# A weight sum formed by an accumulating DMA, one split moved ahead of the other work, and attention's first weights spread over earlier steps

## The chip, the cores and the metric

One core of a Trainium2 chip runs the whole program. The metric is device time in microseconds of that core. Most of the time is spent by TensorE (PE) on matrix products; VectorE (DVE), ScalarE (ACT) and GpSimd (POOL) prepare operands and add up results, SyncE's queue (SP) and POOL's and ACT's queues issue the DMAs.

## The reference

Two sequences of 512 tokens with 1024 features go through two layers. Layer 0 mixes tokens by a Fourier transform, layer 1 by attention; each is followed by an MLP with a squared ReLU:

```python
for i in range(DEPTH):
    if i % 2 == 0: x = x + fourier_mix(rms_norm(x, fourier_norm), fourier_w_out)
    else:          x = x + gqa_attention(rms_norm(x, attn_norm), w_qkv, ..., w_o)
    a = maximum(rms_norm(x, mlp_norm[i]) @ w_up[i], 0)      # 1024 -> 4096
    x = x + (a * a) @ w_down[i]                             # 4096 -> 1024, "second product"
return rms_norm(x, final_norm)
```

Everything is float32.

## The kernel before, in words

**Three matmuls for one.** A float32 operand is split into two parts of a narrower type: ACT rounds the value to the high part (line 85, `CAST`), DVE subtracts to get the low part (line 86). A product is then three matmuls, high by high, high by low and low by high (line 784 for the MLPs; lines 80 to 82 elsewhere).

**Seven products for eight.** The MLP matrices are cut into 2 x 2 blocks, and a block product is made from seven products of sums of blocks in place of eight. In the second product of a layer (`second_product`) the hidden features lie in four groups of blocks (`g`), the outputs in four (`m`). For each pair (g, m) there is one `Row` (two products, with the plain weight blocks 11 and 12) and one `Sums` (five products: t1 with weight sum s1, t3 with s3, t2 with s2, b22 with s4, t4 with block 22). A product is 12 matmuls of 128x512, or 6 in the one group of layer 1 that has two blocks in place of four.

With a11, a12, a21, a22 the four weight blocks, the sums are s1 = a21 + a22, s2 = s1 - a11, s3 = a11 - a21, s4 = a12 - s2. `Sums.load` brings two raw tiles, x = (a12, a21) and y = (a11, a22). `sum_123` (lines 1058 to 1060) makes s1 and s2 in a third raw tile and s3 in place; `sum_4` (line 1066) makes s4 in place. `split_12` splits s1 and s2 as one tile, `split_4` splits s4, and `split_3` splits s3 and a22 as one tile.

**Items.** The main loop runs over 16 items (rows, sums), one for each (g, m), and mixes in work for the next item. Most items have one row besides the sums, 84 matmuls; the items of (0,0) (whose rows run ahead of the loop), (0,1), (3,2) and (3,3) have none, 60 matmuls. PE's order is written out by hand (`manual_schedule(engines={PE})`). The order of the other engines is fixed when the program is built, by a planner that puts an instruction where its operands and its buffer should be there, the earlier in the program first. Within an item the program says: the row's first product; load of the next row; `split_3` of this item's own sums; t1, load of the next sums; t3, the row's second product, split of the next row; t2, then `sum_123` and `split_12` of the next sums; b22, then `sum_4` and `split_4` of the next sums; t4; and at the end `finish`, which adds the parts up (lines 1129, 1130).

**Buffers.** Raw tiles share five buffers (`rawp`), split weights four (`wp`), and 38 buffers (`act`) hold the activations: 8 for the residual stream, 28 for the seven operands of a group (b11, b21, b22, t1 to t4, four each), which leaves two. Operands come back from memory where the first product spilled them (`fetch`, line 981), and `put` splits them; `change` fetches the next group's operand after its last use.

**End of layer 0.** When the last group is done for a value of m, `ready(m)` scales the result into attention's operand `hT` (`make_h`: ACT line 89, DVE line 90; one `act` buffer for each of four calls) and squares it for the norm (ACT line 160, POOL line 162). Attention's first weights, the four tiles `w_qkv[2, 0..3]` that make keys and values, are loaded and split by `late()` while the last items run. Each takes a raw buffer until it is split, and two `act` buffers. `late()` loads two of them at the start of item (3,2) and two at the start of item (3,3). Attention's first products use hT and these weights.

**Start of a layer's second product.** The first product's last step runs the generator `ahead()`, which fetches the first group's operands and loads the first four rows and the first sums by SP, while POOL still writes the last spills.

Of the kernel before, what the change touches and what calls it, by code (L numbers as in the profile page):

```python
# [11 lines left out]
F32 = mybir.dt.float32  # L12
# [3 lines left out]
ALU = mybir.AluOpType  # L16
AX = mybir.AxisListType

P = 128
# [18 lines left out]
GROUPS = ((0, 4), (4, 4), (8, 4), (12, 4)), ((2, 4), (6, 4), (10, 2), (12, 4))  # L38
# [5 lines left out]
def trunk_kernel(ctx, tc, x_in, xt_in, y_out, dcos, dsin, feat, rope, gfour, gcol, grow, gfin,  # L44
                 w_four, w_nyq, w_qkv, w_o, w_up, w_row2, w_row4, w_sum2, w_sum4, w_down):
    nc = tc.nc
# [3 lines left out]
    rawp = ctx.enter_context(tc.tile_pool(name="rawp", bufs=5))  # L50
# [9 lines left out]
    def nm(s):  # L60
        n_[0] += 1
        return f"{s}_{n_[0]}"

    def slot(shape, dt):
        return act.tile(shape, dt, tag="u4", name=nm("u"))

    def tm(shape=(P, 512), dt=F32):
        return tmp.tile(list(shape), dt, tag="t2", name=nm("t"))

    def small(n=4):  # L70
        return sm.tile([P, n], F32, tag="s", name=nm("s"), padded_shape=[P, 8])
# [12 lines left out]
    def split(dst_hi, dst_lo, src, eng=nc.vector):  # L84
        nc.scalar.copy(dst_hi, src)  # L85
        eng.tensor_sub(dst_lo, src, f32(dst_hi))  # L86
# [5 lines left out]
    def load_raw(src, shape=(P, 1024)):  # L92
        raw = rawp.tile(list(shape), F32, tag="raw", name=nm("raw"))
        nc.sync.dma_start(raw, src)
        return raw
# [17 lines left out]
    def load_w(src, eng=nc.vector, parts=1, home=own):  # L113
        raw = load_raw(src)
        w = home()
        for i in range(parts):
            sl = slice(i * 1024 // parts, (i + 1) * 1024 // parts)
            split(w[0][:, sl], w[1][:, sl], raw[:, sl], eng)
        return w
# [852 lines left out]
    def second_product(l, blocks, rows, late=lambda: None, ready=lambda m: None):  # L972
# [3 lines left out]
        def fetch(op, g, n):  # L976

            h = []
            for k in range(0, n, 2):
                hi, lo = slot([P, 2, 512], F32R), slot([P, 2, 512], F32R)  # L980
                nc.sync.dma_start(f32(lo), spill[l][op][g][k : k + 2].rearrange("n p f -> p n f"))
                h.append((hi, lo))
            return h

        def put(op, h):
            for hi, lo in h:
                split(hi, lo, f32(lo))
            b[op] = b.get(op, []) + [(hi[:, i], lo[:, i]) for hi, lo in h for i in range(2)]
# [11 lines left out]
        def residual(q, m):  # L1000
            if (q, m) not in there:
                xs[q, m] = slot([P, 2, 512], F32)
                nc.sync.dma_start(xs[q, m], park[q, m])
                there.add((q, m))
            return xs[q, m]
# [8 lines left out]
        def sums_raw(m, g, n):  # L1014
            if (1, m, g) in early:
                return early[1, m, g]
            w = w_sum4[GROUPS4.index((l, g)), m] if n == 4 else w_sum2[m]
            return [load_raw(w[:, i : i + 2], (P, 2, n * P)) for i in (0, 2)]

        class Row:  # L1020


            def __init__(self, m, g, n):
                self.m, self.g, self.n = m, g, n

            def load(self):
                residual(0, self.m)
                self.raw = None if self.m in rows_early else row_raw(self.m, self.g, self.n)
# [15 lines left out]
        class Sums:  # L1044


            def __init__(self, m, g, n):
                self.m, self.g, self.n, self.o = m, g, n, {}

            def load(self):  # L1050
                for q in range(NSEQ):
                    residual(q, self.m)
                self.x, self.y = sums_raw(self.m, self.g, self.n)

            def sum_123(self):
                a21, a11, a22 = self.x[:, 1], self.y[:, 0], self.y[:, 1]
                s = self.s = rawp.tile([P, 2, self.n * P], F32, tag="raw", name=nm("raw"))
                nc.vector.tensor_add(s[:, 1], a21, a22)
                nc.vector.tensor_sub(s[:, 0], s[:, 1], a11)
                nc.vector.tensor_sub(a11, a11, a21)  # L1060

            def split_12(self):
                self.s2, self.s1 = halves(self.s, self.n * P, (own, narrow)[self.n == 2])
# [62 lines left out]
        def finish(m):  # L1126
            left[m] -= 1
            if left[m] == 0:
                nc.vector.tensor_add(xs[0, m][:, 1], xs[0, m][:, 1], e[m])
                nc.vector.tensor_add(xs[1, m], xs[1, m], e[m].unsqueeze(1).broadcast_to([P, 2, 512]))  # L1130
                ready(m)
# [13 lines left out]
        def change(op, g):  # L1145

            if g + 1 < len(GROUPS[l]):
                later.append([0, op, g + 1, fetch(op, g + 1, GROUPS[l][g + 1][1])])

        rows, sums = items[0]  # L1150
        items[0] = [], sums
        with tc.manual_schedule(engines={ET.PE, ET.Activation, ET.DVE}):
            for r in rows:
                r.load()
                r.split()
            sums.load()
            rows[0].first()
            rows[1].first()
            put(*there_later[0])
            sums.sum_123()  # L1160
            sums.sum_4()
            rows[2].first()
            rows[3].first()
            for r, step in zip(rows, (sums.split_12, sums.split_4, sums.split_3, lambda: None)):
                r.second()
                step()
            for r in rows:
                finish(r.m)

        def hook():  # L1170
            for x in later:
                x[0] += 1
            if later and later[0][0] > 2:
                _, op, g, h = later.pop(0)
                b.pop(op, None)
                put(op, h)
                held[op] = g

        for k, (rows, sums) in enumerate(items):
            nrows, nsums = items[k + 1] if k + 1 < len(items) else ([], None)  # L1180
            if sums.g == len(GROUPS[l]) - 1 and sums.m > 1:
                late()
            with tc.manual_schedule(engines={ET.PE}):
                for r in rows:
                    r.first()
                    if r.m == 3:
                        change("b11", r.g)
                for r in nrows:
                    r.load()
                if k:  # L1190
                    sums.split_3()
                hook()
                for i, op in enumerate(("t1", "t3", "t2", "b22", "t4")):
                    sums.go(i)
                    if sums.m == 3:
                        change(op, sums.g)
                    if i == 0 and nsums:
                        nsums.load()
                    if i == 1:
                        for r in rows:  # L1200
                            r.second()
                            if r.m == 3:
                                change("b21", r.g)
                        hook()
                        for r in nrows:
                            r.split()
                    hook()
                    if k == 0 and i in (2, 4):
                        change(ROW[i // 4], 0)
                    if i == 2 and nsums:  # L1210
                        nsums.sum_123()
                        nsums.split_12()
                    if i == 3 and nsums:
                        nsums.sum_4()
                        nsums.split_4()
            for r in rows:
                finish(r.m)
            finish(sums.m)


    hT, rs, wkv = [[], []], [], []
# [5 lines left out]
        rs.append(r)  # L1227

    def late():
        for _ in range(2):  # L1230
            wkv.append(load_w(w_qkv[2, len(wkv)], home=lent))

    def ready(m):
        for q in range(NSEQ):
# [3 lines left out]
            put_away(q, m)  # L1238

    second_product(0, blocks, rows, late, ready)  # L1240

    gb = tm((P, 4, HD))
# [115 lines left out]
    for cg in (2, 0, 1):  # L1358
        ws = wkv if cg == 2 else [load_w(w_qkv[cg, u], home=own if u < 2 else lent) for u in range(4)]
        for q in range(NSEQ):  # L1360
# [6 lines left out]
            for t in range(NT if (cg, q) != (1, 1) else 2):  # L1367
# [11 lines left out]
                if cg == 2:  # L1379
                    raw = tm((P, 256))  # L1380
# [3 lines left out]
                else:  # L1384
                    raw = tm()
# [7 lines left out]
    raw, ss = slot([P, 1024], F32), small(8)  # L1393
# [30 lines left out]
    for kh in range(2):  # L1424
        ahead += [load_w(w_o[k], home=lent) for k in range(len(ahead), 4 * kh + 4)]
        ws = ahead[4 * kh :]
        for q in range(NSEQ):
            if kh == 0:
                load_xs(q, park[q])
            for fo in range(KC):  # L1430
# [13 lines left out]
                if (q, fo) > (1, 4):  # L1444
                    blocks.first_lo(fo - 5)
    blocks.first_lo(3)
    second_product(1, blocks, ())
    ats = []
    for f in range(2 * PLAIN):
        raw = load_raw(plain[f], (P, 2, 512))  # L1450
# [263 lines left out]
```

## Time and profile before

| | us |
|---|---|
| median of 3 runs | 1725.88 (1724.98 to 1727.17) |
| the profiled execution | 1728.54 |
| its span, first to last instruction | 1726.8 |
| PE busy in the span | 1677.5 (97%) |
| DVE busy | 1260.5 (73%) |
| ACT busy | 865.7 (50%) |
| POOL busy | 349.3 (20%) |

Times in the rows are microseconds from the start of the span. A matmul's busy time in the profile covers its way through the array, so that neighbours overlap; how fast PE really goes is seen from how many matmuls start in a stretch. A row of the timeline has the start, the length, the engine, the line, the operation, the tiles (out<-in), the count, and in brackets how long the engine stood idle before it and what released it.

### The profile page before, as it was taken

Reading aid. Unit: us, or ns where it says so; the run is one execution under the profiler, and the core shown is the slowest. Engines: PE = TensorE matmul, PEld = TensorE weight load, DVE = VectorE, ACT = ScalarE, POOL = GpSimd, SP = SyncE. Lnnn points to the kernel's source line nnn. Section 1 sums busy time; section 2 is a strip of 40 time slices with the busy share of each in tenths; the row PEclk is TensorE's granted clock in tenths of the full one; section 3 lists DMA queues with packets and bytes.
Section 4 is the critical chain, followed back from the end, with each engine's and each line's share of the span. In section 5 each row is a group of like instructions: output and inputs, shape, how many; then the busy total and the mean of one; then the engine's idle time right before and its main releaser. Section 6 shows DMA issues by size and latency. Waiting matters only on the chain. (4 is left out here: it accounts for less than half of the span.)

```text
span 1726.8 us, 21966 instructions
## 1 busy us (share of the span) xinstructions
PE 1677.5 (97%) x7846; PEld 1393.1 (81%) x7846; DVE 1260.5 (73%) x1871; ACT 865.7 (50%) x1530; POOL 349.3 (20%) x312
## 2 busy tenths in 40 slices
PE   4999999999999999999999999999999999999997
PEld 4888888888788888788887888788888887888887
DVE  8778777555878869975578844697765578879865
ACT  6666444445442435546687724564444562434334
POOL 3330444222000000412234302102432210000004
PEclk8999999999999999999999999999999999999999
DMA  8833455349654545430100212224543593535322
GB/s 282 220 111 122 153 203 199 141 155 343 257 189 153 195 146 197 154 107 25 49 25 1 90 57 98 110 102 166 195 172 140 203 399 123 201 130 214 137 98 98
DMA packets 103350, 266.06 MB, mean 154 GB/s; under 512 B 10169, under 2 KB 10169, under 8 KB 103241
## 3 DMA queue, kind: packets, MB, share of 16 engines
q1 hardware_dynamic: 86760, 231.63, 37.3%
q10 hardware_dynamic: 14112, 25.70, 3.9%
q0 software_dynamic: 2368, 7.34, 2.0%
q8 instruction: 61, 1.00, 0.2%
q14 instruction: 49, 0.39, 0.1%
HBM read 189.66 MB, written 73.92 MB: 153 GB/s over the span
## 5 line engine op out<-in xcount | busy, mean ns | idle before, releaser
L784 PE MATMUL ps<-u,w 128*128 128x512 f32 x4656 | 1072.0, 391 | 8.5 <-DVE w L86 6.6
L784 PEld LDWEIGHTS ps<-u,w 128*128 128x128 f32 x4656 | 874.2, 188 | 197.6 <-DVE w L86 11.2
L85 ACT CAST w<-raw 128x1024 fp32r<-128x1024 f32 (+1 forms) x224 | 218.3, 980 | 373.8 <-PE ps L784 247.1
L86 DVE TENSOR_TENSOR w<-raw,w 128x1024 fp32r<-128x1024 f32 (+1 forms) x224 | 261.2, 1169 | 81.1 <-ACT w L85 80.7
L162 POOL TENSOR_TENSOR t<-t,t 128x512 f32<-128x512 f32 (+1 forms) x56 | 80.2, 1436 | 705.7 <-ACT t L160 650.1
L86 DVE TENSOR_TENSOR u<-u,u 128x1024 fp32r<-128x1024 f32 x131 | 160.9, 1256 | 21.1 <-ACT u L85 21.0
L80 PE MATMUL ps<-u,u 128*128 128x512 f32 (+2 forms) x424 | 162.9, 385 | 2.4 <-DVE u L577 1.6
L81 PE MATMUL ps<-u,u 128*128 128x512 f32 (+2 forms) x424 | 157.5, 372 | 5.2 <-DVE u L86 5.1
L82 PE MATMUL ps<-u,u 128*128 128x512 f32 (+2 forms) x424 | 157.7, 372 | 2.1 <-POOL u L86 1.6
L85 ACT CAST u<-u 128x1024 fp32r<-128x1024 f32 x131 | 130.6, 1042 | 50.2 <-PE ps L784 35.4
L991 DVE TENSOR_TENSOR u<-ps,u 128x512 f32<-128x512 f32 x160 | 109.7, 687 | 53.6 <-PE ps L784 53.0
L784 PE MATMUL ps<-u,u 128*128 128x512 f32 x552 | 132.0, 390 | 1.1 <-DVE t L868 1.1
L901 POOL TENSOR_TENSOR u<-u 128x512 f32<-128x512 f32 x28 | 36.5, 1304 | 431.7 <-ACT u L798 431.7
L784 PEld LDWEIGHTS ps<-u,u 128*128 128x128 f32 x552 | 103.5, 188 | 23.3 <-issue 1.9
L797 ACT ACTIVATE t<-t 128x512 f32<-128x512 f32 x64 | 40.4, 631 | 115.9 <-DVE t L868 105.3
L81 PEld LDWEIGHTS ps<-u,u 128*128 128x128 f32 x424 | 82.8, 195 | 17.4 <-DVE u L86 7.2
L82 PEld LDWEIGHTS ps<-u,u 128*128 128x128 f32 x424 | 82.3, 194 | 15.9 <-POOL u L86 2.2
L80 PEld LDWEIGHTS ps<-u,u 128*128 128x128 f32 x424 | 82.8, 195 | 14.8 <-DVE u L577 2.1
L86 DVE TENSOR_TENSOR u<-ps,u 128x512 fp32r<-128x512 f32 (+4 forms) x126 | 76.6, 627 | 18.0 <-ACT u L85 16.7
L85 ACT CAST u<-ps 128x512 fp32r<-128x512 f32 (+4 forms) x126 | 66.5, 541 | 25.2 <-PE ps L82 14.7
L768 DVE TENSOR_TENSOR u<-ps,u 128x512 f32<-128x512 f32 (+1 forms) x48 | 30.9, 644 | 60.9 <-PE ps L82 60.9
L857 DVE TENSOR_TENSOR t<-ps,u 128x512 f32<-128x512 f32 x32 | 22.0, 688 | 60.7 <-PE ps L784 57.3
(220 smaller groups left out, 2021.7 us busy)
## 6 DMA issues: line engine op xcount, KB each, us to landing
raw<-w_up SPq DMA_DIRECT2D x80, 512.0 KB, 4.3
u<-spill_t SPq DMA_DIRECT2D x60, 512.0 KB, 6.6
raw<-w_sum SPq DMA_DIRECT2D x56, 512.0 KB, 3.7
u<-spill_b SPq DMA_DIRECT2D x45, 512.0 KB, 6.5
spill_t<-u SPq DMA_DIRECT2D x84, 256.0 KB, 2.0
spill_b<-t ACTq DMA_DIRECT2D x60, 256.0 KB, 4.2
raw<-w_row SPq DMA_DIRECT2D x28, 512.0 KB, 3.3
park<-u SPq DMA_DIRECT2D x24, 512.0 KB, 3.0
```

Of the source, the lines that this page charges most:

```text
L80: nc.tensor.matmul(out, lh, rh, start=first, stop=False)
L81: nc.tensor.matmul(out, lh, rl, start=False, stop=False)
L82: nc.tensor.matmul(out, ll, rh, start=False, stop=last)
L85: nc.scalar.copy(dst_hi, src)
L86: eng.tensor_sub(dst_lo, src, f32(dst_hi))
L162: nc.gpsimd.tensor_add(acc[q][:, :n], acc[q][:, :n], s[:, :n])
L768: nc.vector.tensor_add(x[:, :n], o[:, :n], x[:, :n])
L784: nc.tensor.matmul(o, w[x][:, sl], h[k][y], start=first and k + i == 0, stop=k == n - 1 and i == 2, skip_group_check=not first)
L797: nc.scalar.activation(t, src, AF.Relu)
L857: nc.vector.tensor_add(u2, ob, t[:, 0])
L901: eng.tensor_sub(t[:, 0], b12, b11)
L991: nc.vector.tensor_add(x, o, x)
```

## The change

1. `s1` is no longer added by DVE. `sums_raw` takes a third raw tile `s` at the load, SP loads a21 into its second half, and a DMA issued by POOL adds a22 to it in place (`accum_op=ALU.add`). `sum_123` becomes `sum_23`: s3 = a11 - a21 in place, s2 = a22 - s3. The tile s is thus taken when x and y are, ahead of both, and not when the sums are made; a21 and a22 are read from memory a second time.
2. `split_3` of the next sums stands behind t4 of the item before, ahead of `finish`, and not in the next item behind its row's first product.
3. `late()` loads one tile at a time: one at the start of item (3,0), two in item (3,1) behind the row's second product, one at the start of item (3,2).

The diff, cut to its core:

```diff
 def sums_raw(m, g, n):
     ...
-    return [load_raw(w[:, i : i + 2], (P, 2, n * P)) for i in (0, 2)]
+    s = rawp.tile([P, 2, n * P], F32, tag="raw", name=nm("raw"))
+    nc.sync.dma_start(s[:, 1], w[:, 1])
+    nc.gpsimd.dma_start(s[:, 1], w[:, 3], accum_op=ALU.add)
+    return [s] + [load_raw(w[:, i : i + 2], (P, 2, n * P)) for i in (0, 2)]
 ...
-            def sum_123(self):
+            def sum_23(self):
                 a21, a11, a22 = self.x[:, 1], self.y[:, 0], self.y[:, 1]
-                s = self.s = rawp.tile([P, 2, self.n * P], F32, tag="raw", name=nm("raw"))
-                nc.vector.tensor_add(s[:, 1], a21, a22)
-                nc.vector.tensor_sub(s[:, 0], s[:, 1], a11)
                 nc.vector.tensor_sub(a11, a11, a21)
+                nc.vector.tensor_sub(self.s[:, 0], a22, a11)
 ...
-            if sums.g == len(GROUPS[l]) - 1 and sums.m > 1:
+            end = sums.m if sums.g == len(GROUPS[l]) - 1 else -1
+            if end in (0, 2):
                 late()
 ...
-                if k:
-                    sums.split_3()
                 hook()
                 for i, op in enumerate(("t1", "t3", "t2", "b22", "t4")):
 ...
                             if r.m == 3:
                                 change("b21", r.g)
+                        if end == 1:
+                            late()
+                            late()
                         hook()
                         for r in nrows:
                             r.split()
+                    if i == 4 and nsums:
+                        nsums.split_3()
                     hook()
 ...
     def late():
-        for _ in range(2):
-            wkv.append(load_w(w_qkv[2, len(wkv)], home=lent))
+        wkv.append(load_w(w_qkv[2, len(wkv)], home=lent))
```

More of the change, by code (lines that the diff above doesn't have):

```diff
@@ L1052, in load @@
                     residual(q, self.m)
-                self.x, self.y = sums_raw(self.m, self.g, self.n)
-            def sum_123(self):
+                self.s, self.x, self.y = sums_raw(self.m, self.g, self.n)
+            def sum_23(self):
                 a21, a11, a22 = self.x[:, 1], self.y[:, 0], self.y[:, 1]
-                s = self.s = rawp.tile([P, 2, self.n * P], F32, tag="raw", name=nm("raw"))
-                nc.vector.tensor_add(s[:, 1], a21, a22)
-                nc.vector.tensor_sub(s[:, 0], s[:, 1], a11)
                 nc.vector.tensor_sub(a11, a11, a21)
+                nc.vector.tensor_sub(self.s[:, 0], a22, a11)
             def split_12(self):
@@ L1159, in second_product @@
             put(*there_later[0])
-            sums.sum_123()
+            sums.sum_23()
             sums.sum_4()
@@ L1210, in second_product @@
                     if i == 2 and nsums:
-                        nsums.sum_123()
+                        nsums.sum_23()
                         nsums.split_12()
```

## The prediction

> **What bounds the kernel now.** I read the page first.
>
> ```profile
> PE 1677.5 (97%) x7846; PEld 1393.1 (81%) x7846; DVE 1260.5 (73%) x1871; ACT 865.7 (50%) x1530; POOL 349.3 (20%) x312
> ```
>
> PE is busy 97% of the span, so nothing that is taken off another engine counts by itself; it counts where PE waits for that engine. Then the windows, cut at the second products (422 to 737 in layer 0, 1397 to 1658 in layer 1); the columns are start:end, length, busy time and count of PE, PEld, DVE, ACT, POOL, granted clock, DMA share, GB/s. Under them, a row from the chain of waits.
>
> ```profile
> 460.00:466.00 6.00, 5.00 (x21) 3.42 (x20) 6.00 (x8) 2.52 (x3) 0.00 (x0) 1.00 0.27 87
> 466.00:666.60 200.60, 200.60 (x887) 166.13 (x886) 160.07 (x196) 73.47 (x78) 0.00 (x0) 1.00 0.50 175
> 666.60:685.70 19.10, 19.10 (x86) 15.83 (x85) 18.76 (x24) 7.97 (x10) 0.00 (x0) 1.00 0.36 124
> 685.70:704.70 19.00, 19.00 (x86) 15.73 (x85) 16.89 (x21) 8.30 (x12) 4.98 (x3) 1.00 0.43 161
> 704.70:718.00 13.30, 13.30 (x61) 11.00 (x60) 13.30 (x16) 9.06 (x13) 6.00 (x4) 1.00 0.26 101
> 718.00:726.00 8.00, 4.20 (x17) 2.82 (x16) 8.00 (x10) 1.67 (x3) 1.25 (x2) 1.00 0.85 292
> 726.00:730.00 4.00, 4.00 (x12) 3.15 (x11) 4.00 (x6) 4.00 (x7) 3.92 (x3) 0.57 0.70 263
> 1434.00:1441.00 7.00, 6.00 (x26) 4.22 (x25) 7.00 (x9) 3.02 (x4) 0.00 (x0) 1.00 0.26 81
> 1441.00:1656.00 215.00, 215.00 (x950) 178.06 (x949) 181.50 (x243) 78.49 (x89) 0.00 (x0) 1.00 0.47 164
> ...
> 1439.89 192.96 PE ps L784 x850
> ```
>
> 192.96 us for 850 matmuls is 0.227 us each, and that is what PE does when nothing holds it up. 466 to 666.6 has 887 matmuls, which need 201 us of 200.6; 1441 to 1656 has 950, 216 us of 215. So in the steady part of both second products PE never waits, and an add taken from DVE there is worth nothing. There are three places where PE falls short. 718 to 730 holds 29 matmuls, 6.6 us of work in 12: 5.4 us lost. 460 to 466 holds 21, 4.8 in 6: 1.2 lost. 1434 to 1441 holds 26, 5.9 in 7: 1.1 lost. In all three DVE is busy to the last tenth. These 7.7 us are what the change can win.
>
> The timeline shows the first place, which is the last item of layer 0, (3,3); DVE's rows, then PE's:
>
> ```profile
> 714.88 1.21 DVE L86 TENSOR_TENSOR u<-raw,u 128x1024 fp32r<-128x1024 f32 x1
> 716.01 0.68 DVE L991 TENSOR_TENSOR t<-ps,t 128x512 f32<-128x512 f32 x1
> 716.61 1.21 DVE L86 TENSOR_TENSOR u<-raw,u 128x1024 fp32r<-128x1024 f32 x1
> 717.74 2.30 DVE L86 TENSOR_TENSOR w<-raw,w 128x1024 fp32r<-128x1024 f32 x1
> ...
> 721.17 1.21 DVE L1130 TENSOR_TENSOR u<-u,t 128x1024 f32<-128x1024 f32 x1
> 722.30 0.68 DVE L991 TENSOR_TENSOR u<-ps,u 128x512 f32<-128x512 f32 x1
> 722.90 0.73 DVE L90 SCALAR_TENSOR_TENSOR u<-u,gc,u 128x512 fp32r<-128x512 f32 x1
> 723.56 0.68 DVE L1129 TENSOR_TENSOR u<-u,t 128x512 f32<-128x512 f32 x1
> 724.16 1.21 DVE L86 TENSOR_TENSOR w<-raw,w 128x1024 fp32r<-128x1024 f32 x1
> ...
> 720.10 3.06 PE L784 MATMUL ps<-u,w 128*128 128x512 f32 x12 [1.52 <-DVE w L86]
> 725.43 10.79 PE L784 MATMUL ps<-u,w 128*128 128x512 f32 x39 [2.28 <-DVE w L86]
> ```
>
> t1 waits until 720.10 for s1's low part (717.74). Two L86 that write u stand ahead of it: attention's weights. t3 waits until 725.43 for s3's low part (724.16); ahead of it stand `finish` (L1130, L1129) and an L90 of `ready(2)`. Afterwards the clock is granted at half for a while (0.57 over 726 to 730).
>
> The second product's start, in layer 0 (layer 1 repeats it):
>
> ```profile
> 462.31 1.22 DVE L86 TENSOR_TENSOR u<-u,u 128x1024 fp32r<-128x1024 f32 x1
> 463.44 1.82 DVE L86 TENSOR_TENSOR w<-raw,w 128x512 fp32r<-128x512 f32 x2
> ...
> 465.32 15.04 PE L784 MATMUL ps<-u,w 128*128 128x512 f32 x65 [1.00 <-DVE w L86]
> ```
>
> The clock is full here and PE stops shortly twice. Item (0,1) has no row, so s3 has only t1's 2.7 us (12 x 0.227) between the release of its weight buffer by the former t4 and its use; an operand's split (L86 on u) and s4's go first.
>
> **Part by part.** *Attention's weights sooner.* A split costs DVE 1.21 us (714.88). Two of four stood in item (3,2), where DVE is busy 13.30 of 13.30, and two later. Now one goes into (3,0), where DVE has 0.34 us free, and two into (3,1), with 2.11 free. Those items don't stop PE: their weights are split a product or more ahead. For the last split, `late()` at (3,2), two `act` buffers are wanted when three tiles hold six, so I expect it, and one hT call, only after t1 of (3,3) has released four. (3,2) then loses 2 x 1.21 = 2.4 us of DVE work ahead of s1's split, against the 1.5 us that t1 waited: this wait goes. Each tile's load on SP now goes ahead of the next sums' loads and holds one of five raw buffers until it is split; that delays those loads by one release, which the 19.4 us below cover in (3,1) and (3,2). ACT's part of a split, 1.04 us (711.13 below), finds ACT busy 7.97 of 19.10 and 8.30 of 19.00.
>
> *split_3 sooner.* s3's low part passes ahead of L1130, L90 and L1129 (together 2.6 us); t3 waited 2.28. This wait goes too. What is late next: the adds and hT calls that were passed, first wanted by attention's products 13.6 us (60 x 0.227) later. Cover enough.
>
> So of the 5.4 us I take 5.0, with 0.4 left for a short wait. If the half clock follows the waits, it goes with them; that is in the 5.4, 1.3 of it (4 us less 12 x 0.227). The Trainium skill, "TensorE: Matmul & The Clock Gate", Part 1, says that the clock falls to half after a whole idle window of about 3.4 us. Here the longest wait was 2.28 us and the clock still fell, so the row speaks against that reading; by the page the half clock would have another cause and stay, and the sum would be 1.3 us smaller.
>
> *At the starts.* The add that goes frees 0.6 us of DVE ahead of the wait, and s3 may pass the operand's split ahead of it (1.22). I take 0.8 of 1.2 and of 1.1: 1.6 in all.
>
> *The sum by DMA.* Each `Sums` issues one SP DMA more and one on POOL. Durations, with the steady rhythm under them:
>
> ```profile
> u<-xt POOLq DMA_DIRECT2D x4, 512.0 KB, 8.4
> raw<-w_sum SPq DMA_DIRECT2D x8, 256.0 KB, 2.6
> ...
> u<-u POOLq DMA_DIRECT2D x4, 256.0 KB, 4.3
> ...
> 417.15 3.41 DVE L86 TENSOR_TENSOR u<-u,u 128x1024 fp32r<-128x1024 f32 x2
> 418.28 1.70 POOL L794 DMA_DIRECT2D spill_t<-u  x3
> ...
> 489.35 3.04 SPq L94 DMA_DIRECT2D raw<-w_sum  x2
> ...
> 508.77 1.06 ACT L85 CAST w<-raw 128x1024 fp32r<-128x1024 f32 x1 [1.70 <-PE ps L784]
> ...
> 698.80 2.07 SPq L94 DMA_DIRECT2D raw<-w_sum  x2
> ...
> 711.13 1.04 ACT L85 CAST w<-raw 128x1024 fp32r<-128x1024 f32 x1
> ```
>
> First half 2.6, issue 0.57 (1.70 / 3), the adding DMA 4.3 (the four `u<-u`, the same size and also accumulating) to 8.4 (`u<-xt`, accumulating, twice the size): 7.5 to 11.6 us; I take 7.5. In the steady part the load starts at 489.35 and the split at 508.77, 19.4 us later: hidden from both ends. For (3,3), with loads near 699 to 700, s1 is whole at 707 to 712; the split began at 711.13 and must begin by about 716.3 for a t1 due at 718.6 (720.10 less the wait of 1.52; 1.04 + 1.21 us of splitting). Hidden, with 4 to 9 us over. Behind the adding DMA POOL queues only L162 of `ready`, for which nobody on PE's path waits. The data read twice is 256 KB a `Sums`, where the DMA share of an item is 0.3 to 0.5 (windows above); I take nothing for it.
>
> The Trainium skill, "SBUF — State Buffer", under "SBUF: two separate sides", warns of the opposite: POOL can't write the descriptors of its DMAs while DVE runs in a two-port mode. By this the sum would come only after a DVE gap, which (3,2) doesn't have, and the wait would be rival 2's. The three issues at 418.28 took 0.57 us each while DVE subtracted without a pause (417.15 to 420.56), so I take no blocking.
>
> *Sum:* 5.0 + 1.6 = 6.6 us. The profiled execution took 1728.54 (span 1726.8 and 1.7 around it), 2.7 above the median of the timed runs. 1728.54 - 6.6 = 1721.9; on the median, 1725.88 - 6.6 = **1719.3**.
>
> **Rivals.** *1. The DVE work only moves.* (3,0) and (3,1) have 2.45 us of DVE free, and three splits are 3.6; `ready(1)`'s L90 still meet POOL's adds. If s1's split still ends near 720, t1's wait and its share of the half clock stay, and only t3's 2.28 and part of the clock go: about 3.0 gained, 1722.9. Against it: only 1.2 us is missing, and the 2.4 us leave (3,2) itself.
>
> *2. The third buffer (slower).* s is taken at the load, so that x and y wait for one more release, and s1 needs two DMAs in sequence. At a layer's start y comes a buffer later:
>
> ```profile
> raw<-w_sum SPq DMA_DIRECT2D x2, 512.0 KB, 11.2
> ...
> 422.44 3.01 PE L784 MATMUL ps<-u,u 128*128 128x512 f32 x12 [0.55 <-DVE t L868]
> ...
> 424.48 1.21 DVE L86 TENSOR_TENSOR w<-raw,w 128x1024 fp32r<-128x1024 f32 x1
> ...
> 434.81 0.68 DVE L1058 TENSOR_TENSOR raw<-raw,raw 128x512 f32<-128x512 f32 x1
> ...
> 442.61 1.22 DVE L86 TENSOR_TENSOR w<-raw,w 128x1024 fp32r<-128x1024 f32 x1
> ...
> 708.16 5.05 POOL L162 TENSOR_TENSOR t<-t,t 128x512 f32<-128x512 f32 x3 [13.41 <-ACT t L160]
> ```
>
> Loaded at 425.7 (when the second row's split, 424.48, frees its buffer) and landing in 11.2 us (the pair in 1391 to 1401, with the DMA engines full), y is there at 436.9, 2.1 after 434.81; less the add, 1.5. s1's split would end at 445.3 where 442.61 + 1.22 = 443.8 was; t1 is due at 422.44 + 96 x 0.227 = 444.2. A wait of 1.1, in each layer 2.2. At the end, if (3,3)'s s must wait for (3,2)'s y, it starts near 705 (where the window of (3,2) begins), its first half lands at 707.5, POOL is in its adds until 713.2, and with 0.57 + 8.4 s1 is whole at 722.2, split at 724.4: t1 waits 5.8, and 1.3 goes to the clock, 7.1 against 5.4. Then +1.7 + 2.2 = +3.9, 1729.8. It decides if s1 is whole later than 716.3. For it: five raw buffers for s, x, y and up to two others. Against it: 4 to 9 us of slack, and the 9 us between L1058 and s1's split at the start hold only some 4 us of work.
>
> **How the numbers follow.** A measurement of this kernel can tell about 0.2% (3.5 us) from no change. The forecast and its neighbours (gains over 3.5) get 0.66, rival 1 and other partial gains 0.15, rival 2 and like losses 0.19. The low end is all 7.7 won, 1718.2, less 1.2 for the spread of runs: 1717.0. The high end takes in rival 1 and most of no change and small losses: 1728.5; left out above it are rival 2's full price and worse.
>
> **What would show it.** Right: 718 to 732 has matmuls every 0.227 us and a clock of 1.00; "PE L784 <- DVE w L86" falls from several us to under 2; L86 on u<-raw appears near 670 and near 698; attention's first product starts some 5 us sooner. Wrong: PE waiting on L85 or L86 of w in (3,3) with the adding DMA landing just before; a wait at the first t1 of a layer, near 444 or 1419; or a new DVE wait in (3,0) to (3,2).

## The result, and the profile after

The changed kernel takes 1721.39 us (median of 7 runs, 1719.24 to 1722.84) where the kernel before, timed beside it, takes 1726.62 (1724.89 to 1728.43). The ratio is 0.9971, 95% interval 0.996 to 0.9983: 5.2 us faster, 0.29%. The forecast was 1719.3, 6.6 us faster. The profiled execution took 1721.07.

The page, its first lines:

```profile
span 1719.3 us, 22138 instructions
PE 1675.5 (97%) x7846; PEld 1392.5 (81%) x7846; DVE 1239.4 (72%) x1839; ACT 866.1 (50%) x1530; POOL 378.1 (22%) x344
```

DVE has 32 instructions and 21.1 us less, POOL 32 DMA issues more. The windows after, with the columns as before (start:end, length, PE, PEld, DVE, ACT, POOL, granted clock, DMA share, GB/s):

```profile
460.00:466.00 6.00, 6.00 (x29) 4.95 (x28) 6.00 (x8) 2.20 (x3) 0.00 (x0) 1.00 0.87 225
466.00:666.60 200.60, 200.60 (x887) 166.10 (x886) 153.78 (x186) 74.89 (x80) 8.69 (x10) 1.00 0.65 207
704.70:718.00 13.30, 13.30 (x60) 11.02 (x59) 12.13 (x14) 7.56 (x11) 7.16 (x4) 1.00 0.60 194
718.00:730.00 12.00, 11.88 (x50) 8.95 (x49) 11.95 (x15) 8.17 (x13) 4.86 (x3) 1.00 0.76 254
1430.00:1441.00 11.00, 11.00 (x50) 9.13 (x49) 10.82 (x14) 1.57 (x2) 0.86 (x1) 1.00 0.64 213
1555.00:1600.00 45.00, 43.78 (x193) 35.58 (x192) 38.20 (x55) 19.58 (x24) 2.16 (x3) 1.00 0.76 255
```

The three places of the forecast have closed: PE is busy 6.00 of 6.00 in the first row (5.00 before), 11.88 of 12.00 in the fourth, at full clock (8.20 before, half of it at 0.57), and 11.00 of 11.00 at the start of layer 1. The last row is new: 45 us in the group of layer 1 that has two blocks. Before, PE was busy there throughout and started 200 matmuls:

```profile
1555.00:1600.00 45.00, 45.00 (x200) 37.28 (x199) 43.12 (x67) 16.91 (x22) 0.00 (x0) 1.00 0.61 216
```

Now it starts 193. The steady part (second row) still has its 887 matmuls, though the DMA share went from 0.50 to 0.65.

DVE's timeline at the end of layer 0 shows attention's weights (L86, u<-raw) moved, and the last of them behind the low parts that t1 and t3 need:

```profile
667.66 1.22 DVE L86 TENSOR_TENSOR u<-raw,u 128x1024 fp32r<-128x1024 f32 x1
...
695.27 2.35 DVE L86 TENSOR_TENSOR u<-raw,u 128x1024 fp32r<-128x1024 f32 x2
...
711.34 1.72 DVE L86 TENSOR_TENSOR w<-raw,w 128x1024 fp32r<-128x1024 f32 x1
...
717.10 1.23 DVE L1132 TENSOR_TENSOR u<-u,t 128x1024 f32<-128x1024 f32 x1
718.24 1.22 DVE L86 TENSOR_TENSOR w<-raw,w 128x1024 fp32r<-128x1024 f32 x1
...
721.11 0.74 DVE L90 SCALAR_TENSOR_TENSOR u<-u,gc,u 128x512 fp32r<-128x512 f32 x1
721.77 1.22 DVE L86 TENSOR_TENSOR u<-raw,u 128x1024 fp32r<-128x1024 f32 x1
722.91 0.68 DVE L1131 TENSOR_TENSOR u<-u,t 128x512 f32<-128x512 f32 x1
```

And here is what the forecast did not have: DVE's and PE's waits, with what they waited for (us in total, times, longest), and the loads (count, size, median us from issue to landing).

```profile
DVE raw L1061 <- DMA raw<-w_sum: 30.5, 16, 3.4
...
PE ps L784 <- DVE t L991: 1.2, 2, 0.8
...
raw<-w_sum SPq DMA_DIRECT2D x56, 512.0 KB, 5.0
raw<-w_sum SPq DMA_DIRECT2D x36, 256.0 KB, 4.6
raw<-w_sum POOLq DMA_DIRECT2D x28, 256.0 KB, 5.7
```

The same rows of the kernel before (its add of s1 was L1058):

```profile
DVE raw L1058 <- DMA raw<-w_sum: 0.9, 1, 0.9
...
raw<-w_sum SPq DMA_DIRECT2D x56, 512.0 KB, 3.7
```

DVE waited 0.9 us in all for x and y, and their 512 KB landed in 3.7 us. Now it waits 30.5 us, at the subtraction that makes s3 (L1061), more than the 32 adds of some 0.66 us (21.1 in all) that the change saves it. Almost all of this lies beside PE's work. In the short group it doesn't, as the timeline of DVE and PE there shows:

```profile
1585.51 0.69 DVE L1061 TENSOR_TENSOR raw<-raw,raw 128x512 f32<-128x512 f32 x1 [2.33 <-DMA raw<-w_sum]
...
1587.99 0.68 DVE L991 TENSOR_TENSOR t<-ps,t 128x512 f32<-128x512 f32 x1
...
1564.48 5.74 PE L784 MATMUL ps<-u,u 128*128 128x512 f32 x24 [0.39 <-DVE t L991]
...
1588.72 3.02 PE L784 MATMUL ps<-u,w 128*128 128x512 f32 x12 [0.83 <-DVE t L991]
```

DVE stands 2.33 us before a subtraction, in its order the product's L991 comes behind, and PE, whose products are 6 matmuls (1.4 us) here, waits until L991 has taken a product out of `ps`. By the starts of the matmuls the two gaps lose 0.55 and 0.99 us.

### The profile page after: what moved, and what is told of

It reads as the page before. It is cut to its first block, busy times and chain, and to the rows that moved or that the text cites. A ratio compares the mean times of both kernels' runs of the same rounds, so it can differ in the third digit from the quotient of the medians.

```text
span 1719.3 us, 22138 instructions
## 1 busy us (share of the span) xinstructions
PE 1675.5 (97%) x7846; PEld 1392.5 (81%) x7846; DVE 1239.4 (72%) x1839; ACT 866.1 (50%) x1530; POOL 378.1 (22%) x344
## 5 line engine op out<-in xcount | busy, mean ns | idle before, releaser
L86 DVE TENSOR_TENSOR w<-raw,w 128x1024 fp32r<-128x1024 f32 (+1 forms) x224 | 260.1, 1165 | 84.3 <-ACT w L85 83.9
L86 DVE TENSOR_TENSOR u<-u,u 128x1024 fp32r<-128x1024 f32 x131 | 161.3, 1257 | 16.6 <-ACT u L85 16.0
L991 DVE TENSOR_TENSOR u<-ps,u 128x512 f32<-128x512 f32 x160 | 109.3, 684 | 39.5 <-PE ps L784 37.0
L1020 POOL DMA_DIRECT2D raw<-w_sum x32 | 27.9, 871 | 468.1 <-DVE w L86 235.8
L86 DVE TENSOR_TENSOR u<-ps,u 128x512 fp32r<-128x512 f32 (+4 forms) x126 | 76.5, 626 | 18.8 <-ACT u L85 17.5
```

Of the source, the lines that this page charges most:

```text
L991: nc.vector.tensor_add(x, o, x)
L1020: nc.gpsimd.dma_start(s[:, 1], w[:, 3], accum_op=ALU.add)
```

## The experiments

For each kernel, the us that PE lost at the four places (gaps over 0.2 us between the starts of neighbouring matmuls, less 0.227, half clock included), worked out from the trace, and the timed ratio. The kernel before took 1726.2 to 1727.2 us beside them.

| | starts, layer 0 / 1 | end of layer 0 | short group | us | ratio (95%) |
|---|---|---|---|---|---|
| before | 1.17 / 1.17 | 5.5 | 0 | | 1 |
| changed | 0 / 0 | 0.3 | 1.5 | 1721.39 | 0.9971 (0.996 to 0.9983) |
| e1: weights' move alone | 1.17 / 1.17 | 0 | 0 | 1720.71 | 0.9961 (0.9948 to 0.9975) |
| e2: split_3's move alone | 1.17 / 1.17 | 1.7 | 0 | 1722.96 | 0.9979 (0.997 to 0.9989) |
| e3: sum by DMA alone | 0 / 0 | 4.8 | 3.9 | 1724.35 | 0.9983 (0.9975 to 0.9992) |
| e4: both moves, no sum by DMA | 1.17 / 1.16 | 0 | 0 | 1721.02 | 0.9964 (0.9951 to 0.9976) |
| e5: changed, x and y loaded first | 0 / 0 | 0.5 | 1.2 | 1722.19 | 0.997 (0.9959 to 0.9981) |
| e6: changed, short group adds by DVE | 0 / 0 | 1.3 | 0 | 1718.52 | 0.9951 (0.9939 to 0.9964) |
| e7: weights' move and sum by DMA | 0 / 0 | 0.8 | 1.0 | 1721.76 | 0.9973 (0.9962 to 0.9983) |
| e8: changed, a22 added by DVE from y | 0.70 / 0.69 | 0.3 | 0 | 1720.64 | 0.9962 (0.9949 to 0.9974) |
| e9: changed, sum by DMA in group 0 alone | 0 / 0 | 0 | 0.2 | 1716.03 | 0.9944 (0.9931 to 0.9958) |
| e10: as e9, split_3 at its old place | 0 / 0 | 0 | 0 | 1717.64 | 0.9952 (0.994 to 0.9965) |
| e11: changed, a22 loaded by SP, added by DVE | 0.64 / 0.64 | 0.9 | 0.5 | 1720.21 | 0.9968 (0.9955 to 0.998) |
| e12: as e11, a22 loaded by POOL | 0.70 / 0.69 | 0.6 | 0.8 | 1723.37 | 0.9978 (0.9969 to 0.9987) |

An interval is some 2 us to each side, so the verdicts on single places come from the traces, one profiled execution of each kernel. The times agree in sign but for e3: by its places it loses 0.9 us more than the kernel before (8.7 against 7.8), by the times it is 2.5 us faster (1.4 to 4.3). What makes the difference is open; other stretches of these executions differ too (see e9).

**The three parts, each alone.** e1 has only point 3 of the change, e2 only point 2, e3 only point 1; their diffs are those parts of the diff above.

> Only the attention weights are moved (one tile at (3,0), two in (3,1), one at (3,2)); s1 is still added by DVE and split_3 stands where it stood. Theory A (the two moves win, the sum by DMA wins next to nothing and costs about 1.7 us in the short group of layer 1): t1's wait in (3,3) goes, t3's wait of some 2.3 us and the two waits at the starts of the second products stay; 2 to 3.5 us faster than before, no new wait in layer 1's short group. Rival B (the add taken off DVE is what makes room): the splits that are put into (3,0) and (3,1) push the sums back, less than 1 us of change. Half clock: if it needs both waits it is not granted here; if one wait of 2.3 us is enough it stays.

> Only split_3 is moved. Theory A: t3's wait in (3,3) goes, t1's of 1.5 us stays; at the starts of both second products the longer wait (1.2 us) mostly goes, since s3 passes the operand's split; 2.5 to 4.5 us faster than before. Rival B: at the starts nothing changes without the add taken off, and in (3,3) the adds and hT calls that are passed come back as a wait; less than 2 us faster.

> Only the sum by DMA. Theory A: DVE waits some 30 us in all for the loads of x and y, against 19 us of adds saved; about 1.7 us of PE waits in layer 1's short group (on add_e of t) as in the changed kernel; the waits at (3,3) and at the starts change by 0.6 us each at most; between 1 us faster and 2 us slower than before. Rival B: the starts' waits (2.3 us) and part of (3,3)'s go; 3 us or more faster.

*e1* loses nothing at the end of layer 0 any more, by the weights' move alone: 6.2 us faster, more than theory A's 2 to 3.5. PE's and DVE's timeline show both the starts that stay and why t3's wait went too:

```profile
465.87 4.37 PE L784 MATMUL ps<-u,w 128*128 128x512 f32 x18 [1.00 <-DVE w L86]
...
1434.31 3.92 PE L784 MATMUL ps<-u,w 128*128 128x512 f32 x16 [1.00 <-DVE w L86]
...
711.93 1.72 DVE L86 TENSOR_TENSOR w<-raw,w 128x1024 fp32r<-128x1024 f32 x1
...
719.21 1.21 DVE L86 TENSOR_TENSOR w<-raw,w 128x1024 fp32r<-128x1024 f32 x1
...
722.74 1.22 DVE L86 TENSOR_TENSOR u<-raw,u 128x1024 fp32r<-128x1024 f32 x1
723.87 0.68 DVE L1129 TENSOR_TENSOR u<-u,t 128x512 f32<-128x512 f32 x1
```

s3's split (719.21) stands ahead of L1129 and of three hT calls though `split_3` is where it was: without attention's weights before t1, the planner has it there by itself. In the changed kernel it stands in the same order (717.10 L1132, then 718.24).

*e2* takes t3's wait and leaves t1's, and against theory A the starts' waits stay whole. At the end of layer 0 one row of waiting is left, and no half clock behind it:

```profile
718.96 13.48 PE L784 MATMUL ps<-u,w 128*128 128x512 f32 x58 [1.52 <-DVE w L86]
```

The two moves are thus not terms of a sum: the weights' takes both waits, split_3's one of the same two. *e3* takes the starts' waits and nothing else does. DVE's timeline at the start of layer 0, then PE's two long waits and their windows:

```profile
456.34 1.83 DVE L86 TENSOR_TENSOR w<-raw,w 128x1024 fp32r<-128x1024 f32 x2
458.09 0.68 DVE L991 TENSOR_TENSOR u<-ps,u 128x512 f32<-128x512 f32 x1
458.69 1.21 DVE L86 TENSOR_TENSOR w<-raw,w 128x1024 fp32r<-128x1024 f32 x1
459.82 1.22 DVE L86 TENSOR_TENSOR u<-u,u 128x1024 fp32r<-128x1024 f32 x1
...
719.76 12.32 PE L784 MATMUL ps<-u,w 128*128 128x512 f32 x46 [2.35 <-DVE w L86]
...
1590.19 4.58 PE L784 MATMUL ps<-u,w 128*128 128x512 f32 x12 [2.20 <-DVE t L991]
...
719.00:727.00 8.00, 7.24 (x25) 5.91 (x26) 7.81 (x8) 7.42 (x12) 6.88 (x4) 0.79 0.62 224
1590.00:1594.00 4.00, 3.81 (x10) 3.05 (x11) 4.00 (x6) 0.00 (x0) 0.00 (x0) 0.57 0.85 316
```

Before, the operand's split (u<-u) came first and the weights' two followed; without the add it comes behind them. In e2, with the add, it still comes first and PE still waits. The same kernel loses 3.9 us in the short group, a wait of 2.20 with a half clock behind it. Neither theory of e3 holds whole: the starts' waits went, as in rival B, but only 0.7 us of (3,3)'s 5.5, and the short group lost more than theory A gave it.

**Two parts together.** e4 leaves point 1 out, e7 leaves point 2 out.

> Both moves, s1 still added by DVE. Theory A: 5 us at (3,3), 1 to 3 at the starts, no loss in the short group: 6 to 8 us faster than before, as fast as the changed kernel or 1 to 2 us faster than it. Rival B: without the add taken off DVE, (3,0) to (3,2) don't hold the moved splits; 2 to 4 us faster than before, slower than the changed kernel.

> The changed kernel without the move of split_3. If that move does nothing beside the other two (the earlier runs: the weights' move alone took both waits of (3,3), the sum by DMA alone both at the starts): the same as the changed kernel within 1 us, first MLP unchanged. If split_3 sooner is what keeps the short group's loss at 1.5 us (the sum by DMA alone lost 2.4 there and a half clock after it): 2 to 3 us slower than the changed kernel, with a wait near 1590.

*e4* is as fast as the changed kernel: 1721.02. PE's waits for weights are 2.8 us, those of the starts among them; nothing is lost in the short group.

```profile
PE ps L784 <- DVE w L86: 2.8, 5, 1.0
```

So by the places the sum by DMA gives 2.3 us at the starts and takes 1.5 in the short group. The times don't show that balance: e1, without the sum by DMA and without split_3's move, has 0.9961 where the changed kernel has 0.9971, and the intervals overlap. *e7* without split_3's move equals the changed kernel within the intervals, place by place within 0.6 us.

**Where the loss comes from.** e5 issues x's and y's loads ahead of those of s. e6 lets the group of two blocks add by DVE again:

```diff
# e5
+xy = [load_raw(w[:, i : i + 2], ...) for i in (0, 2)]
 s = rawp.tile(...)
 ...
-return [s] + [load_raw(w[:, i : i + 2], ...) for i in (0, 2)]
+return [s] + xy
# e6 (in e9: "if g" and "if self.g" in place of n == 2)
+if n == 2: return [None] + [load_raw(w[:, i : i + 2], ...) for i in (0, 2)]
 ...
+if self.n == 2: # sum_123 as before
# e8
-nc.gpsimd.dma_start(s[:, 1], w[:, 3], accum_op=ALU.add)
 ...
+nc.vector.tensor_add(self.s[:, 1], self.s[:, 1], a22)
```

> The changed kernel with one order turned: x and y take their buffers and are loaded first, s last. Theory C (the loss in layer 1's short group comes from x and y waiting one buffer release longer): DVE's waits for loads of w_sum fall from some 30 us to a few, the two PE waits of 0.55 and 0.99 us in the short group go, the rest stays: 1.5 us faster than the changed kernel, 6.5 to 8 faster than before. Rival D (the adding DMA is too slow for the short group): s1 comes later still, ACT waits for it at the split of s1, the PE waits stay or grow: as the changed kernel or 1 to 3 us slower.

> The changed kernel, but in layer 1's group of two blocks s1 is added by DVE as before, with no third buffer at the load. Both C and D: the two PE waits there go (1.5 us); the starts stay without waits, since they are in groups of four: 6.5 to 8 us faster than before. If the waits stay, they belong to the order that split_3's move gives there.

> The changed kernel with s still taken at the load and a21 loaded into it by SP, but a22 added by DVE and not by POOL's DMA: the buffer without the adding DMA. Theory C: DVE waits for the loads as in the changed kernel, PE waits of 1.5 us or more in the short group, and the add is back, so 1.2 us at each start: 2.5 to 4 us slower than the changed kernel. Rival D: no waits in the short group; only the starts are worse, 1 us slower than the changed kernel.

*e5:* DVE's waits fall from 30.5 to 3.6 us, but s is late now, and ACT, which rounds it, waits. Nothing is won:

```profile
ACT w L85 <- DMA raw<-w_sum: 35.8, 7, 9.4
ACT u L85 <- DMA raw<-w_sum: 7.3, 2, 5.7
```

*e6* has no loss in the short group, though DVE still waits 24.5 us, almost all of it in the other groups. It is 2.9 us faster than the changed kernel by the medians, but only 0.5 by the places, since it loses 1.0 more at the end of layer 0. DVE's rows there, then PE's:

```profile
703.33 0.69 DVE L1069 TENSOR_TENSOR raw<-raw,raw 128x512 f32<-128x512 f32 x1 [2.00 <-DMA raw<-w_sum]
...
715.61 1.22 DVE L86 TENSOR_TENSOR w<-raw,w 128x1024 fp32r<-128x1024 f32 x1
...
716.88 9.33 PE L784 MATMUL ps<-u,w 128*128 128x512 f32 x37 [0.90 <-DVE w L86]
```

DVE waits 2.00 us for a load, then works without a pause of over 0.04 us until 716.83, where s3's low part is ready that PE waits for. So the waits cost PE where a product is 6 matmuls; where it is 12 most of them cost nothing, but not here, where DVE has no pause left to catch up in. *e8* keeps the third buffer and has no accumulating DMA: no loss in the short group, 14.0 us of DVE's waits. The third buffer, with a21 read twice, does half of the waiting and none of the short group's loss. With the add back on DVE, 0.7 of the 1.17 returns at each start.

**The sum only where it pays.**

> The changed kernel, with the accumulating DMA only in the first group of three blocks; the group of two blocks adds s1 by DVE as before. Theory A (the sum by DMA is worth 2.6 us where the products are long, 24 matmuls, and costs 1.5 us where they are short): in the first group of both layers no wait at the start (gaps of 1.17 us gone), no loss in layer 1's short group, and no waits at the end of layer 0: 1718.0 to 1719.0 us, ratio 0.9945 to 0.9957, as in the run in which the short group adds by DVE. Theory B (the changed kernel's loss in the short group is what its first group leaves behind, a queue of late loads): the short group loses 1.0 to 1.5 us still, 1720.5 to 1721.5 us.

> As the run before it, but split_3 at its old place. Theory A (split_3's move adds nothing beside the weights' move): the same time within 0.7 us, 1718.0 to 1719.2 us, and no gap over 0.6 us at the end of layer 0. Theory B (split_3's move is needed when DVE does the adds of the short group): one gap of 1.0 to 2.3 us at t3 of the last block, 1720 to 1722 us.

("Three blocks" and "24 matmuls" in the first text are slips: group 0 has four blocks, a product 12 matmuls.) *e9* is the fastest kernel of the study by its median, 1716.03 us, 10.2 below the kernel before beside it. Its interval is clear of the changed kernel's, but overlaps those of e1, e4, e6 and others. PE goes without a stop through the first start and through the end of layer 0, and waits 0.8 us for weights in the whole run:

```profile
439.81 30.54 PE L784 MATMUL ps<-u,w 128*128 128x512 f32 x134
...
699.79 26.91 PE L784 MATMUL ps<-u,w 128*128 128x512 f32 x118
...
PE ps L784 <- DVE w L86: 0.8, 3, 0.5
```

The four places account for 7.6 of its 10.2 us. The rest is not explained by the change: where no code differs, the profiled executions differ too. From PE's first matmul to the first MLP they took 97.8 us here, 100.1 in the kernel before and 101.1 in e11, and at the first MLP's start the kernel before has a half clock that e9 has not (rows below, under the half clock). How often such stretches come in the timed runs, no run here shows. *e10* loses nothing at the four places either: no gap at t3 with split_3 at its old place. In these kernels the move of split_3 is not needed.

**What makes x and y late.** Both kernels bring the same bytes as the changed one. a22 is loaded into the other half of s and added by DVE:

```diff
# e11 (e12: nc.gpsimd in place of nc.sync)
-nc.gpsimd.dma_start(s[:, 1], w[:, 3], accum_op=ALU.add)
+nc.sync.dma_start(s[:, 0], w[:, 3])
 ...
+nc.vector.tensor_add(self.s[:, 1], self.s[:, 1], self.s[:, 0])
```

> The changed kernel's loads, all of them, but a22 is loaded to the operand that it had before and added by DVE: the same bytes on the queues and the same third buffer, without POOL's accumulating DMA. Theory C (the extra traffic of the loads makes x and y late): the operand's 512 KB land in about 5.0 us, DVE waits some 25 to 30 us for them, and the short group of layer 1 loses 1 to 1.5 us. Theory D (the accumulating DMA itself does it): 512 KB land in about 4.3 us, DVE waits about 14 us, and no loss in the short group. Time 1720.5 to 1722.5 us by C, 1719.5 to 1721 us by D.

> The changed kernel's loads once more, a22 to the operand by a plain DMA that POOL issues, and DVE adds it: as the run with this load on SP's queue, but on the queue that the changed kernel uses, without the accumulation. Theory E (a load on POOL's queue runs beside those on SP's and slows them): the operand's 512 KB land in about 5.0 us, DVE's waits for x and y come to 25 to 30 us and layer 1's short group loses some 1.5 us: 1721 to 1722.5 us. Theory F (the accumulation itself does it: it reads and writes the tile that it adds to): as on SP's queue, about 4.3 us and 11 us, and no loss over 0.6 in the short group: 1719.5 to 1721 us.

DVE's waits and the landing of x and y in e11, where L1062 makes s3:

```profile
DVE raw L1062 <- DMA raw<-w_sum: 10.8, 13, 1.9
...
raw<-w_sum SPq DMA_DIRECT2D x56, 512.0 KB, 4.3
```

and in e12:

```profile
DVE raw L1062 <- DMA raw<-w_sum: 17.6, 14, 2.9
DVE raw L1061 <- DMA raw<-w_sum: 11.3, 13, 1.4
raw<-w_sum SPq DMA_DIRECT2D x56, 512.0 KB, 4.0
```

On SP's queue the extra bytes cost x and y no more than e8's (4.3 us, 11 us of waits): traffic alone is not the cause, and most of the short group's loss is gone (0.5 of 1.5 us is left). On POOL's queue, without accumulation, they land in 4.0 us, so the queue does not lengthen their loads; yet DVE waits 17.6 us for them and 11.3 for a22, and 0.8 us are lost. The landing of 5.0 comes with the accumulation, where it is issued ahead of x and y (in e5, behind them, they land in 4.1 and DVE waits 3.6). Neither theory holds alone. Why x and y come later in e12 with a landing of 4.0 stays open, as does its median (1723.37 of 11 runs, 1720.04 to 1725.88, where the profiled execution took 1720.9).

## Why the prediction was right or wrong

**Right: what bounds the kernel.** An add taken from DVE in the steady part was worth nothing, and the gain came from the three places named, which closed.

**Attention's weights.** Right, and larger than put down: the splits came at 667.66, at 695.27 and, for the last, at 721.77, behind t1, as expected; t1's wait went. DVE has 1.2 us free in (3,2) where it had none, but 1.1 of it is a wait for x and y (at 705.95); in e1, without that wait, it is as full as before (13.27 of 13.30). So these windows show another order of DVE's work, and no room won. One sign named for being wrong thus came, a new DVE wait in (3,2), and PE didn't feel it here, as it did in e6. The step that failed is the split of the 5.0 us between this part and the next: e1 shows that it wins all 5.5.

**split_3.** "t3 waited 2.28. This wait goes too" is true of this part alone (e2: 1.7 us left of 5.5), but beside the other it wins nothing that the runs can tell (e1 against e4, e7 against the changed kernel, e10 against e9). It passed L1131 and hT calls, and not L1132, which stands ahead of it. The prediction read two waits as two causes with a remedy each; either remedy takes the second wait, and only the weights' move takes the first.

**The half clock.** It went with the waits, as taken. On the Trainium skill, "TensorE: Matmul & The Clock Gate", Part 1, by which the clock falls after a whole idle window of about 3.4 us: e3 has a half clock of 3.4 us (the 0.57 over four) behind a single wait of 2.20 us by the profile, with no wait near it. So the runs speak against the page on how long PE must be idle. They agree with it on the length of what follows. A wait of 1.52 (e2) brought none. But the length of a wait alone doesn't decide. In the profiled executions of the kernel before, e1, e5, e8 and e10 the clock also falls at the start of the first MLP, where PE had waited some 0.8 us at most in the 30 us before, and had then run eight matmuls of 128x2; in the other nine the same waits bring none. The kernel before, then the changed one:

```profile
125.60:129.00 3.40, 3.40 (x10) 2.62 (x9) 2.19 (x7) 0.47 (x3) 0.00 (x0) 0.50 0.00 0
...
126.80:130.20 3.40, 3.40 (x17) 2.80 (x16) 1.97 (x6) 0.28 (x3) 0.00 (x0) 1.00 0.00 0
```

What decides it stays open.

**The starts.** 0.8 each was mis-sized: 1.17 each, and not by split_3, as e2 and e4 show, but by the sum by DMA. The prediction had both effects, the add's 0.6 and the operand's split of 1.22 that s3 passes, which together are more than the 1.17 to be won, and took a value between none and all. With DVE still adding (e8, e11) some 0.5 of each 1.17 is won.

**The sum by DMA.** Its own terms were near enough: 5.7 us to land where 4.3 to 8.4 was the range, 0.87 to issue where 0.57 was taken, and ACT never waited for s. Nor did DVE hold up POOL's issues: the 32 took 0.85 to 0.91 us each, beside a DVE that was busy 72% of the span. The step that failed is "The data read twice ...; I take nothing for it". The range was asked whether s is in time, and not what s does to the loads behind it: x and y land in 5.0 us for 3.7, and DVE waits 30.5 us. Of this, 1.5 us reached PE, in a group that the prediction did not look at, because PE had no wait there. Rival 2 had the mechanism, a third buffer and late loads, but at the layer's start and at (3,3), where 0.3 us was lost and no start was late; e8, with the buffer and without the accumulating DMA, loses nothing in the short group.

**The sum.** 6.6 was predicted; by places it is 5.2 + 2.3 - 1.5 = 6.0, and the timed medians say 5.2 with 2.9 to 6.9 in the interval. The end of layer 0 was right within 0.2; of the two errors, +0.7 at the starts and -1.5 in the short group, one made up for half of the other, and that the sum came out so near is in that part luck. That the change gains over the kernel before is shown by its interval; that it gains over the weights' move alone is not (e1). Rival 1 is out: t1's wait did not stay.

## What to carry to other kernels

When two waits follow each other on one engine's order, try each remedy alone: the first wait's may take both, as e1's did. When work moves from an engine to a DMA, ask of each group of loads what it delays, and look for the group with the shortest products, not only for the one where the engine waits now: the late loads cost 1.5 us beside products of 6 matmuls, and beside products of 12 next to nothing but where DVE had no time left (e6, some 1 us). A change that gains in one group and loses in another can be made in the first alone (e9: 1716.03 us).

## What the runs showed of the hardware

A wait of PE of 2.20 us was followed by 3.4 us at half clock (e3), one of 1.52 was not (e2), and 3.4 us at half clock also came behind waits of 0.79 us at most (the kernel before, at 125.6). An accumulating DMA of 256 KB, issued by POOL, took 0.87 us to issue and 5.7 us to land; a plain one took 0.54 us (17.3 us for 32, e12) and 4.1. Behind the accumulating ones the sums' loads of 512 KB on SP's queue took 5.0 us, behind the plain ones 4.0.
